# First chunk by channel tile and 128-row filter weights in a hybrid encoder trunk

## The chip, the core and the metric

The kernel runs on one core of one Trainium2 chip. The metric is the device time of one execution in microseconds (us), median of three runs. The engines are TensorE (PE; its weight loads are a row of their own, PEld), VectorE (DVE), ScalarE (ACT), GpSimd (POOL) and SyncE (SP), which here only issues DMAs.

## The reference

Two layers on 256 tokens of 1024 channels, in fp32. Cut to what matters here:

```python
def _rms_norm(x, g):
    return x * lax.rsqrt(jnp.mean(x * x, axis=-1, keepdims=True) + 1e-6) * g

for i in range(2):
    proj = _rms_norm(x, norm_mix_pre[i]) @ w_in[i]
    # three mixers on parts of proj: long convolution by FFT, gated linear attention, pooling
    merged = sum(gate_b * (y_b @ w_br_b[i]) for b in ("hyena", "gla", "pool"))
    x = x + _rms_norm(merged @ w_out[i], norm_mix_post[i])
    # gated MLP with a depthwise convolution of width 3, 1024 -> 2816 -> 1024
    x = x + _rms_norm(mlp(_rms_norm(x, norm_ffn_pre[i])), norm_ffn_post[i])

# the long convolution's filter, positions t, features z (33 wide), hidden width 64:
h = sin(fr2 * (sin(fr1 * (z @ w1 + b1)) @ w2 + b2)) @ w3        # (256, 1024)
h_fwd, h_bwd = h[:, :512] * decay, h[:, 512:] * decay
# y = irfft(rfft(x1 * v) * rfft(filter)); y = x0 * (y + x1 * v * bias)
```

## The kernel before

Products are made of three matmuls in the type float32r: an operand is split into an upper part (a copy in that type, by ACT, helper `act`, L98) and a lower part (the rest, by DVE, helper `tt`, L103), and upper by upper, upper by lower and lower by upper are added in PSUM (helper `mm`, L112). The weights, 162 MB with all else, stream from memory in chunks of 1 MB (128 rows by 2048 numbers, tile `raw`, three buffers), 71 a layer, on SP's queue. Each chunk is split in two halves of 1024 columns (`split_upper`, `split_lower`). A unit of matmuls uses a chunk; between units the kernel lets side chains (generators) step and splits chunks ahead.

A scheduler orders each engine's instructions from dependences and its own idea of durations, except between `open_window` and `close_window`: there PE, DVE and ACT (and POOL in the prologue) run in the order in which the code is written. The prologue is such a window. It reaches into the first units of layer 0.

The prologue works so. SP issues in a row: the first 128 tokens of x as two halves of 512 columns (`load_x(0)`), the norm weights `gcol` as 128 rows of 8 numbers, the first half of chunk 0, the other 128 tokens (`load_x(1)`), the second half of chunk 0, chunk 1 (two halves), chunk 2, and `vec`, the table of per-channel constants. PE runs WARM = 13 matmuls of ones (`rmask`) that nobody reads. For the first tokens ACT squares two halves with row sums (`squares`), DVE makes the mean (`mse`), POOL the root (`rstd`, L369), DVE scales x by it (`normed`, L1212), PE transposes eight tiles of 128 channels (L1215), and `gained` multiplies by the norm weight per channel: ACT writes the upper part, DVE the lower one (`stt`, L106), for four channel tiles at a time. The first chunk's halves are split between these steps. Then the same follows for the other tokens, in the generator `second`, which steps as layer 0 begins. `chunk_x_stationary` is a unit of the first product: x is the stationary operand, and for each of four channel tiles k it issues three matmuls of 128x512: upper by upper (m = 0), upper x by lower weights (m = 1), lower x by upper weights (m = 2). In the very first unit `lows_late` puts the m = 1 ones last in each pair of k, so that they come after the other two.

`filt` makes the long convolution's filter. Its hidden state lies twice in `hs`, the upper part in rows 0 to 63 and the lower part in rows 64 to 127, and the weights `w3` lie twice in 128 rows too. For each of two sets of 128 positions and two directions one matmul takes all 128 rows of `hs` against `w3h`, which is upper and lower state by upper weights, and one takes rows 0 to 63 against `w3l`, the lower weights in 64 rows:

```python
w3h, w3l = big.get([P, DM], F32R), big.get([64, DM], F32R)
tt(w3l[:], kf["w3"][0:64, :], f32(w3h[0:64, :]), ALU.subtract)
mm(ps[:], hs[:, w], w3h[:, c], True, False)
mm(ps[:], hs[0:64, w], w3l[:, c], False, True)
```

Later in a layer the inverse transform of the long convolution takes its matrix in two tiles, loaded by POOL's queue (`in_ih` at L804, `in_il` at L805) when buffers come free. The result of a branch, `y`, is written in upper and lower halves and then multiplied by `w_br`.

Of the kernel before, what the change touches and what calls it, by code (L numbers as in the profile page):

```python
# [18 lines left out]
P = 128  # L19
# [57 lines left out]
def trunk(ctx: ExitStack, tc: tile.TileContext, a: dict, out: bass.AP):  # L77
# [9 lines left out]
    def f32(ap):  # L87
        return ap.bitcast(F32)
# [3 lines left out]
    ahead = {"chunks": 3, "reserve": 0, "at": 0, "quiet": False, "still": False}  # L92
    WARM = 13
    TOKEN = "tables"
# [54 lines left out]
    def load_x(t):  # L149
        for s in HALVES:  # L150
            nc.sync.dma_start(xs[t][:, s], a["x"][t * P:(t + 1) * P, s])  # L151

# [8 lines left out]
    gcol = cpool.tile([P, 8], F32, name="gcol")  # L161
    nc.sync.dma_start(gcol[:], a["gcol"])

# [285 lines left out]
    def filt(i, kf):  # L449
        while len(big.free) < 10:  # L450
            yield
        kf["w3"] = big.get([P, DM])
        w3h, w3l = big.get([P, DM], F32R), big.get([64, DM], F32R)
        kf["dec"] = big.get([P, 2, DH])
# [14 lines left out]
        act(w3h[:], kf["w3"][:])  # L469
        tt(w3l[:], kf["w3"][0:64, :], f32(w3h[0:64, :]), ALU.subtract)  # L470
        sml.put(h2)
# [3 lines left out]
        for t in range(2):  # L475
# [4 lines left out]
            for ps, c in ((pf, slice(0, DH)), (pb, slice(DH, DM))):  # L480
                mm(ps[:], hs[:, w], w3h[:, c], True, False)
                mm(ps[:], hs[0:64, w], w3l[:, c], False, True)
            yield
# [49 lines left out]

    def chunk_x_stationary(n, xt, t, o, half, lows_late=False):

        xth, xtl = xt[0][half], xt[1][half]
        s = slice(t * P, (t + 1) * P)
        todo = [(k, m) for k in range(4) for m in range(3)]
        if lows_late:
            todo.sort(key=lambda km: (km[0] // 2, (0, 2, 1)[km[1]]))  # L540
        for k, m in todo:
            h, l = weights(n, k * 512, 512)
            x = xtl if m == 2 else xth
            mm(o, x[:, k, s], l if m == 1 else h, half == 0 and (k, m) == todo[0], half == 1 and (k, m) == todo[-1])
# [22 lines left out]
    def layer(i, xt, chains):  # L567
# [23 lines left out]
        for at, (n, t) in enumerate(seq):  # L591
# [5 lines left out]
            def fin(t=t, ps=vg_ps[t], dst=(v, sg)[m]):  # L597
# [3 lines left out]
            oldest = min(c for c, _ in seq[at:])  # L601
            unit([nvg[n], nvg[oldest]], lambda: chunk_x_stationary(nvg[n], xt, t, vg_ps[t][:], j, lows_late=i == at == 0),
                 fin if j else None, free=nvg[n] if t else None)
# [600 lines left out]
    def squares(t):  # L1204
        h, ss = big.get([P, DM]), ssq_tile()
        for j, s in enumerate(HALVES):
            act(h[:, s], xs[t][:, s], AF.Square, scale=1.0 / 32.0, accum_out=ss[:, j:j + 1])
        return h, ss

    def normed(t, h, r):  # L1210
        for s in HALVES:
            nc.vector.tensor_scalar_mul(h[:, s], xs[t][:, s], r[:])  # L1212
        ps = [psm.get([P, 2, P]) for _ in range(4)]
        for k in range(8):
            nc.tensor.transpose(ps[k // 2][:, k % 2, :], h[:, k * P:(k + 1) * P], ident[:])  # L1215
        big.put(h)
        return ps

    def gained(t, half, ps):
        s = slice(t * P, (t + 1) * P)  # L1220
        for bank in (0, 1):
            b = ps[half * 2 + bank]
# [6 lines left out]
            psm.put(b)  # L1229

    ps = psm.get([P, P])
    for _ in range(WARM):
# [3 lines left out]
    r0 = rstd_mean(ss0)  # L1236
    split_upper()
    ps0 = normed(0, h0, r0)
    gained(0, 0, ps0)
    split_lower()  # L1240
    h1, ss1 = squares(1)
    r1 = rstd_mean(ss1)
    split_upper()
    load_constants()

    def second():
        ps1 = normed(1, h1, r1)
        yield
        gained(1, 0, ps1)
        gained(0, 1, ps0)  # L1250
        split_half(False)
        split_half(False)
        gained(1, 1, ps1)
        ahead["still"] = False
# [147 lines left out]
```

## Time and profile before

| | before |
|---|---|
| median of three runs | 902.9 us (901.14 to 904.99) |
| the profiled execution | 900.64 us |
| its span, first to last instruction | 898.9 us |
| PE busy | 886.0 us (99%) |
| weight loads busy | 830.5 us (92%) |
| DVE busy | 630.9 us (70%) |
| ACT busy | 505.8 us (56%) |
| POOL busy | 35.0 us (4%) |
| moved by DMA | 164.62 MB, mean 183 GB/s |

The profile is of one execution; 1.7 us of its time lie outside the span. An instruction is named by its line, engine, operation, and the tiles it writes and reads (out<-in, buffer numbers left out); `b`, `s` and `p` are slots of the two pools in SBUF and of the one in PSUM. A timeline row gives the start, the length and the count of instructions that it joins, and in brackets the engine's idle time just before and what ended it.

### The profile page before, as it was taken

The numbers are of one execution on the slowest core, as the hardware profiler recorded it, in microseconds if no ns is written. First come the engines' busy times: TensorE is split into PE (matmuls) and PEld (weight loads), VectorE is DVE, ScalarE is ACT, GpSimd is POOL, SyncE is SP. The second block draws the span as 40 slices with busy tenths as digits, with TensorE's granted clock in tenths as the row PEclk, the third lists the DMA queues.
The fourth block names the chain that finished last, engine by engine and source line by source line (L and its number), as shares of the span: only waits on it lengthen the run. The fifth ranks groups of instructions, "written<-read, shape, count | busy, mean of one in ns | idle before, by whom it ended". The sixth has DMA issues, their size and how long they took to land.

```text
span 898.9 us, 15183 instructions
## 1 busy us (share of the span) xinstructions
PE 886.0 (99%) x6272; PEld 830.5 (92%) x6272; DVE 630.9 (70%) x910; ACT 505.8 (56%) x797; POOL 35.0 (4%) x80
## 2 busy tenths in 40 slices
PE   8999999999999999999999999999999999999997
PEld 6899998999988999998888999999998899999885
DVE  5899979665667698765288888865854967776612
ACT  6778746544355776545167865664542766554511
POOL 3000000100010000000010000000000000000000
PEclk9999999999999999999999999999999999999999
DMA  8853545546537426555439545263743583555601
GB/s 290 343 198 129 187 145 178 197 169 246 196 116 268 156 95 240 182 188 205 170 104 337 181 141 198 96 236 141 245 177 141 189 301 125 183 188 178 221 1 47
DMA packets 26021, 164.62 MB, mean 183 GB/s; under 512 B 3178, under 2 KB 3317, under 8 KB 8032
## 3 DMA queue, kind: packets, MB, share of 16 engines
q1 hardware_dynamic: 22464, 151.70, 47.3%
q0 software_dynamic: 3488, 11.95, 4.1%
q8 instruction: 49, 0.80, 0.4%
q14 instruction: 20, 0.16, 0.1%
HBM read 162.59 MB, written 1.05 MB: 182 GB/s over the span
## 4 chain that ended last, share of the span: by engine, by line
PE 96%; DMA 2%; DVE 2%; issue 0%; ACT 0%; SPq 0%; DVEq 0%; POOLq 0%; ACTq 0%
PE p L112 94%; DMA b<-in_il 1%; DVE b L103 1%; DMA raw<-in_wts 1%; PE p L356 1%; PE p L1132 0%; DVE b L106 0%; PE p L749 0%; PE p L965 0%; ACT b L98 0%; SPq L151 0%; DVE s L923 0%; DVE x L106 0%; DVEq L1398 0%; ACT s L98 0%
## 5 line engine op out<-in xcount | busy, mean ns | idle before, releaser
L112 PE MATMUL p<-b,b 128*128 128x256 f32 (+2 forms) x5958 | 854.2, 304 | 5.3 <-DVE b L103 3.5
L112 PEld LDWEIGHTS p<-b,b 128*128 128x128 f32 x5958 | 794.4, 191 | 55.2 <-DVE b L103 4.8
L103 DVE TENSOR_TENSOR b<-raw,b 128x1024 fp32r<-128x1024 f32 x286 | 342.5, 1216 | 123.6 <-ACT b L98 71.2
L98 ACT ACTIVATE b<-raw 128x1024 fp32r<-128x1024 f32 x288 | 290.9, 1045 | 189.1 <-PE p L112 146.7
L103 DVE TENSOR_TENSOR b<-p,b 128x512 f32<-128x512 f32 (+2 forms) x64 | 40.5, 651 | 63.4 <-ACT s L98 51.6
L98 ACT ACTIVATE s<-p 128x256 f32<-128x256 f32 (+3 forms) x50 | 20.5, 414 | 77.5 <-PE p L112 77.2
L98 ACT ACTIVATE b<-p 128x512 f32<-128x512 f32 (+3 forms) x78 | 43.5, 566 | 30.2 <-PE p L112 20.3
L106 DVE SCALAR_TENSOR_TENSOR s<-p,vec,s 128x255 f32<-128x255 f32 x104 | 49.3, 478 | 6.4 <-ACT s L98 5.5
L98 ACT ACTIVATE s<-p,vec 128x256 f32<-128x256 f32 x52 | 28.8, 557 | 18.7 <-DVE s L106 15.3
L98 ACT ACTIVATE s<-s 128x512 f32<-128x512 f32 (+6 forms) x52 | 27.7, 532 | 13.4 <-DVE s L106 8.2
L103 DVE TENSOR_TENSOR b<-b,b 128x512 f32<-128x512 f32 (+4 forms) x34 | 26.6, 781 | 8.3 <-ACT b L98 7.9
L98 ACT ACTIVATE b<-s 128x512 fp32r<-128x512 f32 x38 | 23.7, 625 | 13.1 <-DVE s L103 13.0
L98 ACT ACTIVATE b<-b 128x512 fp32r<-128x512 f32 (+3 forms) x22 | 16.3, 742 | 24.8 <-DVE b L103 23.6
L103 DVE TENSOR_TENSOR b<-s,b 128x512 fp32r<-128x512 f32 x38 | 25.9, 684 | 5.2 <-ACT b L98 5.2
L103 DVE TENSOR_TENSOR b<-b,p 128x512 f32<-128x512 f32 x24 | 16.3, 684 | 10.1 <-PE p L112 9.9
L98 ACT ACTIVATE b<-b,s 128x128 f32<-128x128 f32 x64 | 20.5, 391 | 1.0 <-DVE s L674 0.9
L106 DVE SCALAR_TENSOR_TENSOR b<-p,vec,b 128x255 f32<-128x255 f32 (+1 forms) x40 | 19.1, 477 | 2.6 <-ACT b L98 2.5
L103 DVE TENSOR_TENSOR s<-s,p 128x512 f32<-128x512 f32 x22 | 15.0, 684 | 8.4 <-ACT s L98 8.0
L109 DVE TENSOR_SCALAR mse<-ssq 128x1 f32<-128x1 f32 (+1 forms) x24 | 4.7, 196 | 18.7 <-ACT s L98 14.9
L103 DVE TENSOR_TENSOR s<-s,s 128x512 f32<-128x512 f32 (+2 forms) x24 | 15.6, 662 | 2.0 <-ACT s L98 2.0
L369 POOL TENSOR_TENSOR rstd<-mse,mhalf 128x1 f32<-128x1 f32 x16 | 8.9, 554 | 209.1 <-DVE mse L109 209.1
L112 PE MATMUL p<-b,s 128*128 128x128 f32 (+1 forms) x80 | 15.7, 315 | 0.0
(95 smaller groups left out, 289.8 us busy)
## 6 DMA issues: line engine op xcount, KB each, us to landing
raw<-in_wts SPq DMA_DIRECT2D x140, 1024.0 KB, 5.0
b<-in_gains POOLq DMA_DIRECT2D x7, 512.0 KB, 6.0
raw<-in_wts SPq DMA_DIRECT2D x4, 512.0 KB, 7.3
b<-in_dft POOLq DMA_DIRECT2D x4, 512.0 KB, 7.0
x<-in_x SPq DMA_DIRECT2D x4, 256.0 KB, 4.4
b<-in_gw POOLq DMA_DIRECT2D x2, 512.0 KB, 5.8
b<-in_fw POOLq DMA_DIRECT2D x2, 512.0 KB, 6.7
b<-in_decay POOLq DMA_DIRECT2D x2, 512.0 KB, 8.0
```

Of the source, the lines that this page charges most:

```text
L98: ins = nc.scalar.activation(o, i, func, **kw)
L103: nc.vector.tensor_tensor(out=o, in0=x, in1=y, op=op)
L106: nc.vector.scalar_tensor_tensor(out=o, in0=x, scalar=s, in1=y, op0=op0, op1=op1)
L109: nc.vector.tensor_scalar(out=o, in0=x, scalar1=s1, scalar2=s2, op0=op0, op1=op1)
L112: ins = nc.tensor.matmul(o, w, x, start=start, stop=stop).ins
L356: nc.tensor.transpose(ps[k // 4][:, k % 4, :], h[:, k * P:(k + 1) * P], ident[:])
L369: nc.gpsimd.tensor_tensor(out=r[:], in0=e[:], in1=mhalf[:, 0:1], op=ALU.pow)
```

## The change

- WARM is 9 instead of 13.
- x is loaded with one DMA for each 128 tokens, whole rows of 4 KB.
- The norm weights are loaded as 8 rows of 128 numbers (`grow`), transposed on PE and copied to `gcol` by DVE.
- Of the squares the first 512 columns are on ACT, the other 512 on DVE.
- The scaling is in three pieces (256, 256, 512 columns) and is separate from the transposes (`scaled`, `turned`).
- Chunk 0 is split in quarters of 512 columns, one per channel tile, each between the norm products of two channel tiles.
- The first unit issues k = 0, 1, 2, then the transposes of the other tokens, then k = 3; within k = 1 to 3 the matmul that needs lower weights comes second to last or last.
- In `second` the upper split of chunk 1's first half comes after `gained(1, 0)`, not before.
- `w3l` has 128 rows, and its matmuls take all 128 rows of `hs`: the product of the two lower parts is added, which the kernel before leaves out.

```diff
--- before.py
+++ after.py
@@ -90,7 +90,7 @@
     LIFT = 1000
     newest = {}
     ahead = {"chunks": 3, "reserve": 0, "at": 0, "quiet": False, "still": False}
-    WARM = 13
+    WARM = 9
     TOKEN = "tables"
     TABLED = (AF.Sin, AF.Exp, AF.Ln, AF.Sigmoid, AF.Gelu)
 
@@ -147,8 +147,7 @@
     HALVES = (slice(0, 512), slice(512, 1024))
 
     def load_x(t):
-        for s in HALVES:
-            nc.sync.dma_start(xs[t][:, s], a["x"][t * P:(t + 1) * P, s])
+        nc.sync.dma_start(xs[t][:], a["x"][t * P:(t + 1) * P, :])
 
     def gain(i, j, eng):
         g = big.get([P, DM])
@@ -159,7 +158,8 @@
     g_cur = {}
     load_x(0)
     gcol = cpool.tile([P, 8], F32, name="gcol")
-    nc.sync.dma_start(gcol[:], a["gcol"])
+    grow = cpool.tile([8, P], F32, name="grow")
+    nc.sync.dma_start(grow[:], a["gains"][0, 0].rearrange("(k c) -> k c", c=P))
 
 
     order = []
@@ -450,7 +450,7 @@
         while len(big.free) < 10:
             yield
         kf["w3"] = big.get([P, DM])
-        w3h, w3l = big.get([P, DM], F32R), big.get([64, DM], F32R)
+        w3h, w3l = big.get([P, DM], F32R), big.get([P, DM], F32R)
         kf["dec"] = big.get([P, 2, DH])
         with tc.issue_after(newest["pool"]):
             nc.gpsimd.dma_start(kf["w3"][:], a["fw3"][i])
@@ -467,7 +467,7 @@
         act(hs[:], h2[:])
         tt(hs[64:P, :], h2[64:P, :], f32(hs[64:P, :]), ALU.subtract)
         act(w3h[:], kf["w3"][:])
-        tt(w3l[:], kf["w3"][0:64, :], f32(w3h[0:64, :]), ALU.subtract)
+        tt(w3l[:], kf["w3"][:], f32(w3h[:]), ALU.subtract)
         sml.put(h2)
         big.put(kf["w3"])
         yield
@@ -479,7 +479,7 @@
             w = slice(t, None, 2)
             for ps, c in ((pf, slice(0, DH)), (pb, slice(DH, DM))):
                 mm(ps[:], hs[:, w], w3h[:, c], True, False)
-                mm(ps[:], hs[0:64, w], w3l[:, c], False, True)
+                mm(ps[:], hs[:, w], w3l[:, c], False, True)
             yield
             hf, hb, u = sml.get([P, DH]), sml.get([P, DH]), sml.get([P, DH])
             tt(hf[:], pf[:], kf["dec"][:, t, :], ALU.mult)
@@ -531,14 +531,17 @@
     def xt_alloc():
         return ([big.get([P, 4, L], F32R) for _ in range(2)], [big.get([P, 4, L], F32R) for _ in range(2)])
 
-    def chunk_x_stationary(n, xt, t, o, half, lows_late=False):
+    def chunk_x_stationary(n, xt, t, o, half, first=None):
+
 
         xth, xtl = xt[0][half], xt[1][half]
         s = slice(t * P, (t + 1) * P)
         todo = [(k, m) for k in range(4) for m in range(3)]
-        if lows_late:
-            todo.sort(key=lambda km: (km[0] // 2, (0, 2, 1)[km[1]]))
+        if first is not None:
+            todo = todo[:3] + [(k, m) for k in range(1, 4) for m in (0, 2, 1)]
         for k, m in todo:
+            if first is not None and (k, m) == (3, 0):
+                first()
             h, l = weights(n, k * 512, 512)
             x = xtl if m == 2 else xth
             mm(o, x[:, k, s], l if m == 1 else h, half == 0 and (k, m) == todo[0], half == 1 and (k, m) == todo[-1])
@@ -599,7 +602,8 @@
                 psm.put(ps)
 
             oldest = min(c for c, _ in seq[at:])
-            unit([nvg[n], nvg[oldest]], lambda: chunk_x_stationary(nvg[n], xt, t, vg_ps[t][:], j, lows_late=i == at == 0),
+            unit([nvg[n], nvg[oldest]], lambda: chunk_x_stationary(nvg[n], xt, t, vg_ps[t][:], j,
+                                                                  chains[1].step if i == at == 0 else None),
                  fin if j else None, free=nvg[n] if t else None)
             if at == (5 if i else 3):
                 close_window()
@@ -1203,22 +1207,27 @@
 
     def squares(t):
         h, ss = big.get([P, DM]), ssq_tile()
-        for j, s in enumerate(HALVES):
-            act(h[:, s], xs[t][:, s], AF.Square, scale=1.0 / 32.0, accum_out=ss[:, j:j + 1])
+        s0, s1 = HALVES
+        act(h[:, s0], xs[t][:, s0], AF.Square, scale=1.0 / 32.0, accum_out=ss[:, 0:1])
+        x = xs[t][:, s1]
+        nc.vector.scalar_tensor_tensor(out=h[:, s1], in0=x, scalar=1.0 / 1024.0, in1=x, op0=ALU.mult, op1=ALU.mult,
+                                       accum_out=ss[:, 1:2])
         return h, ss
 
-    def normed(t, h, r):
-        for s in HALVES:
+    def scaled(t, h, r):
+        for s in (slice(0, 256), slice(256, 512), slice(512, 1024)):
             nc.vector.tensor_scalar_mul(h[:, s], xs[t][:, s], r[:])
+
+    def turned(h):
         ps = [psm.get([P, 2, P]) for _ in range(4)]
         for k in range(8):
             nc.tensor.transpose(ps[k // 2][:, k % 2, :], h[:, k * P:(k + 1) * P], ident[:])
         big.put(h)
         return ps
 
-    def gained(t, half, ps):
+    def gained(t, half, ps, banks=(0, 1)):
         s = slice(t * P, (t + 1) * P)
-        for bank in (0, 1):
+        for bank in banks:
             b = ps[half * 2 + bank]
             of = [(xt[0][half][:, k, s], xt[1][half][:, k, s], b[:, k % 2, :], gcol[:, half * 4 + k:half * 4 + k + 1])
                   for k in (2 * bank, 2 * bank + 1)]
@@ -1228,27 +1237,53 @@
                 stt(xl, src, g, f32(xh), ALU.mult, ALU.subtract)
             psm.put(b)
 
+
+    wh[0], wl[0] = ([big.get([P, 1024], F32R) for _ in range(2)] for _ in range(2))
+
+    def upper(k):
+        act(wh[0][k // 2][:, k % 2 * 512:(k % 2 + 1) * 512], raws[0][:, k * 512:(k + 1) * 512])
+
+    def lower(k):
+        s = slice(k % 2 * 512, (k % 2 + 1) * 512)
+        tt(wl[0][k // 2][:, s], raws[0][:, k * 512:(k + 1) * 512], f32(wh[0][k // 2][:, s]), ALU.subtract)
+
     ps = psm.get([P, P])
     for _ in range(WARM):
         mm(ps[:], rmask[:, 0:P], rmask[:, 0:P], True, True)
     psm.put(ps)
     h0, ss0 = squares(0)
     r0 = rstd_mean(ss0)
-    split_upper()
-    ps0 = normed(0, h0, r0)
-    gained(0, 0, ps0)
-    split_lower()
+    psg = psm.get([P, 8])
+    nc.tensor.transpose(psg[:], grow[:], ident[0:8, 0:8])
+    nc.vector.tensor_copy(gcol[:], psg[:])
+    psm.put(psg)
+    scaled(0, h0, r0)
+    ps0 = turned(h0)
+    upper(0)
+    lower(0)
+    gained(0, 0, ps0, (0,))
+    upper(1)
+    lower(1)
+    gained(0, 0, ps0, (1,))
+    upper(2)
+    lower(2)
     h1, ss1 = squares(1)
     r1 = rstd_mean(ss1)
-    split_upper()
+    upper(3)
+    lower(3)
+    scaled(1, h1, r1)
+    del raws[0]
+    dma_next()
+    state["h"] = state["l"] = 2
     load_constants()
 
     def second():
-        ps1 = normed(1, h1, r1)
+        ps1 = turned(h1)
         yield
         gained(1, 0, ps1)
+        split_upper()
         gained(0, 1, ps0)
-        split_half(False)
+        split_lower()
         split_half(False)
         gained(1, 1, ps1)
         ahead["still"] = False
```

The order that each engine gets changes with it. In the first rows of PE before, `b_5` and `b_8` are the scaled x of the two sets of tokens, `b_6`, `b_9` the upper and `b_7`, `b_10` the lower halves of chunk 0, `b_1`, `b_3` the upper and lower x:

```order
L1215 MATMUL p_5_139<-ident,b_5_123 128x128 x2
L112 MATMUL p_6_180<-b_6_131,b_1_103 128x512 x2
L112 MATMUL p_6_180<-b_6_131,b_3_105 128x512 x2
L112 MATMUL p_6_180<-b_7_132,b_1_103 128x512 x2
L112 MATMUL p_6_180<-b_9_165,b_1_103 128x512 x2
L112 MATMUL p_6_180<-b_9_165,b_3_105 128x512 x2
L112 MATMUL p_6_180<-b_10_166,b_1_103 128x512 x2
L1215 MATMUL p_7_201<-ident,b_8_157 128x128 x2
```

In the kernel after these tiles are `b_9` and `b_10` (scaled x), `b_5`, `b_6` (upper) and `b_7`, `b_8` (lower):

```order
L112 MATMUL p_7_189<-b_7_110,b_1_102 128x512
L112 MATMUL p_7_189<-b_6_109,b_1_102 128x512
L112 MATMUL p_7_189<-b_6_109,b_3_104 128x512
L112 MATMUL p_7_189<-b_8_111,b_1_102 128x512
L1224 MATMUL p_8_199<-ident,b_10_162 128x128 x2
L1224 MATMUL p_9_200<-ident,b_10_162 128x128 x2
L1224 MATMUL p_10_201<-ident,b_10_162 128x128 x2
L1224 MATMUL p_11_202<-ident,b_10_162 128x128 x2
L112 MATMUL p_7_189<-b_6_109,b_1_102 128x512
L112 MATMUL p_7_189<-b_6_109,b_3_104 128x512
```

The eight transposes of the other tokens now stand between the ninth and the tenth matmul of the first unit, and each lower part comes with its own channel tile.

ACT in the prologue before, from its second square on (`raw_80` is chunk 0, `raw_85` chunk 1):

```order
L98 ACTIVATE b_8_157,ssq<-x_68 128x512 x2
L98 ACTIVATE b_9_165<-raw_80 128x1024
L98 ACTIVATE b_14_181<-raw_85 128x1024
L98 ACTIVATE b_1_103<-p_7_201,gcol 128x128 x2
L98 ACTIVATE b_1_103<-p_8_202,gcol 128x128 x2
L98 ACTIVATE b_2_104<-p_4_138,gcol 128x128 x2
L98 ACTIVATE b_2_104<-p_5_139,gcol 128x128 x2
```

And after, where `raw_80` is chunk 0 and `raw_84` chunk 1:

```order
L98 ACTIVATE b_6_109<-raw_80 128x512
L98 ACTIVATE b_10_162,ssq<-x_68 128x512
L98 ACTIVATE b_6_109<-raw_80 128x512
L98 ACTIVATE b_1_102<-p_8_199,gcol 128x128 x2
L98 ACTIVATE b_1_102<-p_9_200,gcol 128x128 x2
L98 ACTIVATE b_14_222<-raw_84 128x1024
L98 ACTIVATE b_2_103<-p_5_138,gcol 128x128 x2
L98 ACTIVATE b_2_103<-p_6_139,gcol 128x128 x2
L98 ACTIVATE b_16_234<-raw_84 128x1024
```

The first split of chunk 1 moved behind the first four norm products of the other tokens, and chunk 0's second half is now two steps with one square between them.

In the middle of layer 0, PE just before the first product of the long convolution's result (`b_121`) with its branch weights, before:

```order
L112 MATMUL p_51_1579<-s_34_1456,s_24_1312 128x256
L112 MATMUL p_52_1652<-b_2_104,b_109_1362 128x256
L112 MATMUL p_55_1754<-b_47_434,b_49_436 128x128 x4
L112 MATMUL p_54_1724<-b_121_1488,b_110_1365 128x256
L112 MATMUL p_57_1772<-b_121_1488,b_110_1365 128x256
L112 MATMUL p_54_1724<-b_122_1489,b_110_1365 128x256
```

And after, where `p_53` is the gate product that was `p_52`, and `p_55` the branch product:

```order
L112 MATMUL p_53_1656<-b_2_103,b_108_1365 128x256
L112 MATMUL p_53_1656<-b_4_105,b_108_1365 128x256
L112 MATMUL p_53_1656<-b_2_103,b_109_1366 128x256
L112 MATMUL p_55_1728<-b_121_1492,b_110_1369 128x256
L112 MATMUL p_56_1758<-b_47_438,b_49_440 128x128 x4
L112 MATMUL p_55_1728<-b_122_1493,b_110_1369 128x256
```

Before, one matmul of the gate's product stands there and the product's 47 others ran earlier; after, it is nineteen in a row, of which the last three are shown.

## Rows read from the trace of the kernel before

**Rows 1.** Page, part 4: shares of the span in the chain that ended last, by engine.
```profile
PE 96%; DMA 2%; DVE 2%; issue 0%; ACT 0%; SPq 0%; DVEq 0%; POOLq 0%; ACTq 0%
```

**Rows 2.** TensorE's waits, whole run: us in total, times, longest us.
```profile
PE p L112 <- DVE b L103: 3.5, 3, 2.2
PE p L112 <- ACT b L98: 1.4, 1, 1.4
...
PE p L112 <- DMA b<-in_il: 0.5, 1, 0.5
```

**Rows 3.** Three stretches: us, each engine's busy us and instructions (x), clock, DMA.
```profile
20.00:60.00 40.00, 40.00 (x258) 35.38 (x256) 34.88 (x53) 29.28 (x39) 1.04 (x2) 1.00 0.82 303
60.00:120.00 60.00, 60.00 (x466) 57.56 (x466) 57.33 (x105) 43.98 (x91) 3.09 (x10) 1.00 0.47 166
146.00:892.00 746.00, 746.00 (x5287) 701.54 (x5286) 505.25 (x689) 403.44 (x612) 22.65 (x44) 1.00 0.51 180
```

**Rows 4.** PE timeline, layer 0's filter: start, length, instruction, count, [idle before].
```profile
58.45 1.70 PE L112 MATMUL p<-b,s 128*128 128x512 f32 x4
...
60.66 1.68 PE L112 MATMUL p<-b,s 128*128 128x512 f32 x4
```

**Rows 5.** The same view, weight loads of the first group.
```profile
58.78 0.19 PEld L112 LDWEIGHTS p<-b,s 64*128 64x128 f32 x1 [0.24 <-issue]
59.22 0.19 PEld L112 LDWEIGHTS p<-b,s 128*128 128x128 f32 x1 [0.25 <-issue]
```

**Rows 6.** Groups by form, whole run: count | busy us, mean ns | idle before, releaser.
```profile
L112 PE MATMUL p<-rmask 128*128 128x128 f32 x26 | 5.9, 425 | 1.2 <-DVE rmask L246 1.2
...
L112 PE MATMUL p<-s 128*128 128x128 f32 x32 | 4.9, 275 | 0.0
...
L103 DVE TENSOR_TENSOR b<-b,b 64x1024 fp32r<-64x1024 f32 x2 | 2.4, 1214 | 1.3 <-ACT b L98 1.3
```

**Rows 7.** Timeline of PE, prologue.
```profile
6.89 1.04 PE L1215 MATMUL p<-ident,b 128*128 128x128 f32 x8
...
18.49 5.78 PE L112 MATMUL p<-b,b 128*128 128x512 f32 x24 [0.16 <-DVE b L103]
```

**Rows 8.** Timeline of ACT and DVE, prologue.
```profile
3.44 0.63 ACT L98 ACTIVATE b<-x 128x512 f32<-128x512 f32 x1 [1.42 <-DMA x<-in_x]
...
7.93 1.06 ACT L98 ACTIVATE b<-raw 128x1024 fp32r<-128x1024 f32 x1 [3.11 <-DMA raw<-in_wts]
...
9.53 1.13 DVE L106 SCALAR_TENSOR_TENSOR b<-p,gcol,b 128x128 fp32r<-128x128 f32 x4 [2.92 <-ACT b L98]
...
13.35 0.88 DVE L1212 TENSOR_SCALAR b<-x,rstd 128x512 f32<-128x512 f32 x2
...
14.48 2.18 ACT L98 ACTIVATE b<-p,gcol 128x128 fp32r<-128x128 f32 x8 [1.35 <-PE p L1215]
...
17.22 1.22 DVE L103 TENSOR_TENSOR b<-raw,b 128x1024 fp32r<-128x1024 f32 x1
```

**Rows 9.** DMA view, windows 2 to 3, 3 to 4 and 4 to 5 us.
```profile
raw<-in_wts SPq DMA_DIRECT2D x1, 512.0 KB, 5.8
...
raw<-in_wts SPq DMA_DIRECT2D x1, 512.0 KB, 6.9
...
q1 hardware_dynamic: 66, 0.25, 97.0%
```

**Rows 10.** Timeline of all engines, end of layer 0's long convolution.
```profile
113.49 0.53 POOL L805 DMA_DIRECT2D b<-in_il  x1 [0.79 <-PE p L112]
...
122.54 14.42 PE L112 MATMUL p<-b,b 128*128 128x256 f32 x118 [0.47 <-DMA b<-in_il]
...
142.74 0.47 DVE L923 TENSOR_SCALAR s<-b,s 128x128 f32<-128x128 f32 x2
...
143.13 0.68 DVE L103 TENSOR_TENSOR b<-b,b 128x512 fp32r<-128x512 f32 x1
...
143.86 2.41 PE L112 MATMUL p<-b,b 128*128 128x256 f32 x18 [2.16 <-DVE b L103]
```

## Prediction

> **What bounds the kernel now.** I read the chain of waits first: 96% of it is TensorE (PE) [rows 1]. The view of what PE waits for comes next; the reader is to see how little is left: 3.5 us behind lower halves written by VectorE (DVE), 1.4 behind ScalarE (ACT), 0.5 behind one DMA [rows 2], and 1.2 before its first instruction [rows 6]. From 146 to 892 it is busy throughout [rows 3]: all these waits lie before. So an edit can bring three things only: less time of PE's own instructions, a smaller wait among those few, or (as a loss) a new wait. DVE is the engine that could make one: it is busy 34.88 us of the 40 from 20 to 60, and 57.33 of the 60 from 60 to 120 [rows 3]. The profiled execution took 900.64 us, the median of the runs is 902.9; I sum against the first and scale the result by 902.9/900.64.
>
> **The filter on 128 rows.** Each layer has two groups of four 128x512 matmuls, alternately with 128 rows and with 64. The first group begins at 58.45, and the second, with four 256-wide matmuls between, at 60.66: 2.21 us [rows 4]. Ordinary 128x512 matmuls follow each other by 0.234: 24 of them last 5.78, and (5.78-0.39)/23 leaves out the last one's length [rows 7]; 256-wide ones step by 14.42/118 = 0.122 [rows 10]. So the stretch should take 4x0.234 + 4x0.122 = 1.42, and 0.79 is lost. The loads show where: ahead of the second one, of 64 rows, and of the third, of 128, stands 0.24 and 0.25 of idle with no releaser but issue, and the loads of the other groups read alike [rows 5]. Four groups at 0.8 make 3.2 us, with bounds of 2.4 (two and a half such gaps a group, 0.6) and 3.8 (0.24 at each of sixteen loads). On DVE the lower half of these weights was 64x1024 and took 1.21 us a piece; a 128x1024 one takes 1.22 [rows 6, 8], so the added rows cost nothing there. PE is continuous at this place, so the saving reaches the end unless DVE falls behind (a rival).
>
> The row is the evidence: the idle comes and goes with the number of rows. [...]
>
> **The prologue.** Its end is the point from which PE is continuous: 18.49, when DVE's lower part of chunk 1's first half (17.22, 1.22 long) is done [rows 7, 8]. Back from there stand eight DVE products, ACT's eight from 14.48, eight transposes, the scaling at 13.35 and the squares. All that PE does before 18.49 fits in gaps, so an earlier first matmul is worth nothing by itself. Step by step, for the kernel after:
> - x by whole rows. The first square starts at 3.44 on half the row now; with one transfer I put it at 4.0 (the second half's place). ACT's takes 0.63 and needs its sum read, and DVE's, beside it, I take at 0.68, like its 128x512 step [rows 10]: both end at 4.87, and before two squares in a row from 3.44 ended hardly sooner. Nothing. The bounds of DVE's square are 0.44 (half of the pair of scalings, 0.88) and 0.88 [rows 8].
> - Norm weights by a transpose: one PE transpose, one DVE copy, in the time in which DVE waits for POOL's root. Nothing; under 0.44, one scaling, if that cover were gone [rows 8]. What goes is one DMA on SP's queue ahead of the weights.
> - First weights. Their first half lands 5.8 us after its issue, just ahead of ACT's step at 7.93, the second 6.9 us after its own (at 10.43) [rows 8, 9]. From 4 to 5 us the engines were 97% busy with 66 packets and only 0.25 MB, so it is not small packets that filled them [rows 9]. I take 7.7 and 10.26, 0.2 for the issue that is gone; the early bound is a rival.
> - ACT: a quarter of the upper part 0.56 (half of 1.06, with overhead), two norm products 0.56 (2.18 for eight) [rows 8]. From 7.72: quarter, products, quarter, products to 9.96; third quarter from 10.28 to 10.84; square (0.6) to 11.45; fourth to 12.0.
> - DVE: a quarter 0.64 (half of 1.22, with overhead), two products 0.57 (1.13 for four) [rows 8]. They follow ACT: 8.34 to 10.74; third quarter 10.9 to 11.54; square to 12.22. Root and hand-overs 0.85: scaling at 13.1, against 13.35. It comes in pieces, so the transposes start at 13.45, and ACT's products at 14.05, against 14.48.
> - Then the order gives the lead back: ACT does four products (to 15.15), a half chunk that before was split ahead of them (to 16.15), four products (to 17.2). DVE's eighth product ends at 17.5 and the lower part at 18.7. PE is continuous from 18.8: 0.3 later than 18.49.
>
> So the prologue costs 0.3. Bounds: a loss of 1.5 (transfers 1.0 later, as the two halves differ in their time to landing, and DVE's square at 0.88), a gain of 1.8 (weights that land early). Code that only waits behind other things: `ngb` is put ahead of four products on DVE and waits for `vec`; that DMA no longer stands behind as much, and DVE has waits there; nothing.
>
> **The order in the middle.** The scheduler's order changes as well. Eight matmuls of 0.122 (14.42/118) that stood ahead of the inverse transform now stand behind it. Its second matrix is sent for at 113.49, when PE frees a buffer at the same place in both kernels, so PE reaches it 0.97 earlier and the wait of 0.47 at 122.54 becomes 1.44. In return 0.98 more work stands before the wait of 2.16 at 143.86, for the DVE step at 143.13; and a DVE pair of 0.47 that ran just ahead of that step now runs behind it [rows 10]. That leaves 0.71; one more DVE step, of 0.68, goes ahead of a split there, and I take 0.4. Net 2.16-0.4-0.97 = 0.8 saved; bounds 1.0 lost (nothing gained at the second place) and 2.2 saved. Further on both orders agree up to the end but for the widths in layer 1's filter.
>
> **Sum.** 3.2 + 0.8 - 0.3 = 3.7 saved: 900.64-3.7 = 896.94, scaled 899.2.
>
> **Rivals.**
> [...]
> B, the first weights land early: the small transfer and three issues gone, the stream moves faster than 0.25 MB a microsecond [rows 9], the first half is there before ACT needs it, and by the same steps the second scaling comes at 11.35 rather than 13.1. The prologue gains 1.5 instead of losing 0.3: 5.5 saved, 897.4. Against it: the slow stretch before 8 us does not look like a matter of packet size.
> C, the other side, DVE becomes the bound. It gets about 1.7 us more in the prologue (two squares 1.36, four quarters for two halves 0.28, a copy) and from 20 to 60 it has 40-34.88 = 5.1 idle to take it up. If order and waits eat that, layer 0's filter gains nothing (PE then waits for lower halves), 1.74 appears as waits before 120, and the middle gives only its loss of 1.0: 1.6-1.74-0.3-1.0 = 1.4 lost, 904.4. It decides once DVE runs over 5.1 late at 60.
> D, the width does nothing: the idle at each load belongs to the change of what is read, not of the rows. 3.2 less: 0.5 saved, 902.4. The alternation of rows with an idle at each step [rows 5] speaks against it.
>
> **How the numbers follow.** Chances: forecast 0.42, A 0.20, B 0.20, C 0.08, D 0.05, rest 0.05. A measurement tells about 0.5%, 4.5 us, from no change: below 898.4 is faster, above 907.4 slower. The forecast's own bounds reach below 898.4 in a third of its cases (0.14), B in most (0.16), the others 0.04: faster 0.34; slower 0.04 from the worst of C and the rest; the same 0.62. The range, 895.4 to 902.9, takes in B with the middle's bound of 2.2 (897.4-1.4 = 896.0) and a little of the filter's, and on the other side A and D; it leaves out C and the rest.
>
> **What would show it.** Filter groups: eight rows of 128x512 with steps near 0.23 and no idle at loads; if 0.43 stays, D. [...] A wait near 1.4 for the second inverse matrix and a wait under 0.8 after 135. Any new wait for a lower half between 19 and 120 is C. The prediction is wrong if PE waits after 146, or if instructions that the edit does not touch change in length.

## The result and the profile after

| | before | after |
|---|---|---|
| median, six runs each | 902.76 us | 895.89 us (894.96 to 896.90) |
| ratio to before, 95% interval | | 0.9922 (0.9907 to 0.9938) |
| the profiled execution | 900.64 us | 895.14 us |
| its span | 898.9 us | 893.4 us |
| PE busy | 886.0 us | 882.0 us |

The forecast was 3.7 us less and 899.2; it became 6.9 less by the medians and 5.5 by the two profiled executions. The sign was right, the size not.

What PE waits for in the kernel after, us in total, times, longest (before: [rows 2]):

```profile
PE p L1224 <- DVE b L1219: 2.9, 2, 1.8
PE p L112 <- DVE rmask L246: 1.2, 1, 1.2
PE p L112 <- DVE b L103: 0.5, 1, 0.5
PE p L112 <- ACT b L98: 0.3, 1, 0.3
```

The first row is the prologue, where PE waits for scaled x. The wait for the second inverse matrix is gone, and so is the one of 2.2 for a lower half; one of 0.3 is new, at 78 us.

PE's timeline of the filter after (start, length, instruction, count):

```profile
59.06 1.55 PE L112 MATMUL p<-b,s 128*128 128x512 f32 x6
60.44 2.67 PE L112 MATMUL p<-b,b 128*128 128x256 f32 x21
...
65.22 0.62 PE L112 MATMUL p<-b,s 128*128 128x512 f32 x2
```

The same view, weight loads of the first six:

```profile
58.94 1.24 PEld L112 LDWEIGHTS p<-b,s 128*128 128x128 f32 x6
```

Against [rows 4, 5]: six matmuls take 1.38 up to the next start, 0.23 each, and the loads run without the idle of 0.24. The scheduler split one group, so two stand by themselves.

PE's timeline of the prologue after, against [rows 7]:

```profile
6.70 1.94 PE L1224 MATMUL p<-ident,b 128*128 128x128 f32 x8 [1.10 <-DVE b L1219]
8.29 3.14 PE L112 MATMUL p<-b,b 128*128 128x512 f32 x9
13.24 1.23 PE L1224 MATMUL p<-ident,b 128*128 128x128 f32 x8 [1.80 <-DVE b L1219]
14.22 3.92 PE L112 MATMUL p<-b,b 128*128 128x512 f32 x16
18.65 5.74 PE L112 MATMUL p<-b,b 128*128 128x512 f32 x24 [0.51 <-DVE b L103]
```

Five rows of ACT and DVE from the same stretch, against [rows 8]:

```profile
6.41 0.63 ACT L98 ACTIVATE b<-raw 128x512 fp32r<-128x512 f32 x1 [1.20 <-DMA raw<-in_wts]
...
9.40 0.63 ACT L98 ACTIVATE b<-raw 128x512 fp32r<-128x512 f32 x1 [0.35 <-DMA raw<-in_wts]
...
12.74 1.01 DVE L1219 TENSOR_SCALAR b<-x,rstd 128x256 f32<-128x256 f32 x3 [0.45 <-POOL rstd L369]
...
13.69 1.15 ACT L98 ACTIVATE b<-p,gcol 128x128 fp32r<-128x128 f32 x4 [2.51 <-PE p L1224]
...
17.38 2.35 DVE L103 TENSOR_TENSOR b<-raw,b 128x1024 fp32r<-128x1024 f32 x2
```

Both halves of chunk 0 arrive earlier (6.41 and 9.40 instead of 7.9 and 10.4), the second scaling comes 0.6 earlier, and yet the lower part that ends the prologue starts at 17.38, where before it was 17.22: between lie the half chunk and the eight products in their new order on ACT. Both profiles have 49 of these 128x512 matmuls up to the end of their last row (4+8+13+24 and 9+16+24), at 18.49+5.78 = 24.27 and 18.65+5.74 = 24.39: a loss of 0.12.

At the end of layer 0's long convolution, against [rows 10], PE (two rows) and the DVE step for which it waited 2.16 before:

```profile
138.66 3.53 PE L112 MATMUL p<-b,b 128*128 128x256 f32 x28
...
138.91 0.68 DVE L103 TENSOR_TENSOR b<-b,b 128x512 fp32r<-128x512 f32 x1
```

PE has work throughout; there is no idle. So the profiled executions differ by 3.2 (filter) + 2.16 + 0.47 (two waits) - 0.12 (prologue) - 0.28 (new wait) = 5.4 of the 5.5. The other 1.4 of the medians is not in these two profiles; the experiments point to where it lies.

### The profile page after: what moved, and what is told of

The parts are those of the page before. It is cut to its first block, busy times and chain, and to the rows that moved or that the text cites. A ratio compares the mean times of both kernels' runs of the same rounds, so it can differ in the third digit from the quotient of the medians.

```text
span 893.4 us, 15182 instructions
## 1 busy us (share of the span) xinstructions
PE 882.0 (99%) x6265; PEld 830.3 (93%) x6265; DVE 632.4 (71%) x919; ACT 505.0 (57%) x795; POOL 35.4 (4%) x80
## 3 DMA queue, kind: packets, MB, share of 16 engines
HBM read 162.59 MB, written 1.05 MB: 183 GB/s over the span
## 4 chain that ended last, share of the span: by engine, by line
PE 96%; ACT 1%; DMA 1%; DVE 1%; SPq 0%; issue 0%; POOL 0%; DVEq 0%; POOLq 0%; ACTq 0%
PE p L112 95%; ACT b L98 1%; DMA raw<-in_wts 1%; PE p L356 1%; PE p L1136 0%; ACT s L98 0%; DVE b L103 0%; PE p L969 0%; PE p L753 0%; POOL rstd L369 0%; DVE b L106 0%; SPq L150 0%; DVE x L106 0%; DVEq L1433 0%; DVE b L1213 0%
## 5 line engine op out<-in xcount | busy, mean ns | idle before, releaser
L103 DVE TENSOR_TENSOR b<-raw,b 128x1024 fp32r<-128x1024 f32 (+2 forms) x288 | 342.6, 1209 | 123.4 <-ACT b L98 69.1
L98 ACT ACTIVATE b<-raw 128x1024 fp32r<-128x1024 f32 (+2 forms) x290 | 291.3, 1041 | 179.8 <-PE p L112 143.6
L155 POOL DMA_DIRECT2D b<-in_gains x7 | 3.8, 550 | 269.3 <-PE p L112 157.6
```

What stands on the lines that cost most here:

```text
L98: ins = nc.scalar.activation(o, i, func, **kw)
L103: nc.vector.tensor_tensor(out=o, in0=x, in1=y, op=op)
L155: eng.dma_start(g[:], bass.AP(src.tensor, src.offset + (i * 4 + j) * DM, [[0, P], [1, DM]]))
```

## Experiments

Times are medians beside the kernel before on the same chip, whose median went from 900.9 to 902.6 with the chip, so ratios are compared. The ratios are those on record; the quotient of the two medians differs from them by up to 0.0015.

**The filter alone.** In the kernel before:

```diff
-        w3h, w3l = big.get([P, DM], F32R), big.get([64, DM], F32R)
+        w3h, w3l = big.get([P, DM], F32R), big.get([P, DM], F32R)
...
-                mm(ps[:], hs[0:64, w], w3l[:, c], False, True)
+                mm(ps[:], hs[:, w], w3l[:, c], False, True)
```

> The kernel before with the filter's lower weights on 128 rows and nothing else; every engine's order is that of before. My theory (the switch between 64 and 128 rows costs about 0.2 us a matmul): steps of 0.23 in the four groups, 3.2 us less, 899.6 by the median of before of 902.8; the waits at the second inverse matrix (0.5) and after 141 us (2.2) stay. [...] Rival (DVE takes it back): steps of 0.23, but a new wait for a lower half before 120 us.

Measured: 898.13 against 901.87, ratio 0.9946 (0.9932 to 0.9960). PE's timeline of the two groups:

```profile
57.82 1.09 PE L112 MATMUL p<-b,s 128*128 128x512 f32 x4
58.74 0.64 PE L112 MATMUL p<-b,b 128*128 128x256 f32 x4
59.22 1.09 PE L112 MATMUL p<-b,s 128*128 128x512 f32 x4
```

From group to group 1.40, before 2.21: 0.81 saved, four times 3.2. Nothing was taken back; the waits in the middle (2.2 and 0.4) are as before. The whole time fell by more than 3.2 (3.7 by the medians, 3.6 to 6.1 by the ratio's interval). In this profile the prologue, too, ends 0.6 earlier (17.89 against 18.49), as the first weights came at 7.34 instead of 7.93; so the starts of the groups measure the filter, and the whole time does not.

**The price of the switch.** The kernel before, the same four matmuls in another order:

```diff
                 mm(ps[:], hs[:, w], w3h[:, c], True, False)
+            for ps, c in ((pf, slice(0, DH)), (pb, slice(DH, DM))):
                 mm(ps[:], hs[0:64, w], w3l[:, c], False, True)
```

> The kernel before with the four matmuls of each filter group in another order: two of 128 rows, then two of 64, instead of alternating. If the price is one of a change in the number of rows, two changes a group instead of four: half of the 3.2 us goes, 1.6 less, and the idle of 0.24 ahead of loads stands at two loads of a group. If a 64-row matmul is slow by itself, the idle stays at four loads or sits at the same two matmuls and nothing is saved. The scheduler's order differs a little elsewhere, so the loads are the measure, not the whole time.

Measured: 899.99, ratio 0.9986 (0.9972 to 0.9999). Weight loads:

```profile
58.71 0.31 PEld L112 LDWEIGHTS p<-b,s 64*128 64x128 f32 x2 [0.35 <-issue]
59.37 0.53 PEld L112 LDWEIGHTS p<-b,b 128*128 128x128 f32 x4 [0.35 <-issue]
60.51 0.31 PEld L112 LDWEIGHTS p<-b,s 64*128 64x128 f32 x2 [0.36 <-issue]
61.18 1.97 PEld L112 LDWEIGHTS p<-b,b 128*128 128x128 f32 x16 [0.36 <-issue]
```

Two matmuls of 64 rows in a row, and idle only where the number of rows changes: twice a group instead of four times, 0.35 each. The groups begin at 58.15 and 59.95, 1.80 apart, 0.41 less than 2.21. The price is one of the change, not of a 64-row matmul.

**All but the filter.** The changed kernel with `w3l` on 64 rows:

> The changed kernel with the filter's lower weights on 64 rows again; every engine's order is that of the changed kernel. Theory: the steps of 0.43 are back and 3.2 us with them, 895.9 + 3.2 = 899.1; the waits in the middle of layer 0 stay away. So the rest of the change is worth 902.8 - 899.1 = 3.7, nearly all from the two waits of 0.5 and 2.2. Rival: the filter alone explains the whole gain and the rest is nothing, about 902.8.

Measured: 898.73, ratio 0.9958 (0.9944 to 0.9972). By the medians filter and rest add up: 3.74 and 3.14 are 6.9, the whole. By the ratios they are 4.9 and 3.8 against 7.0, each with an interval of about 1.3 either way, which allows the sum but does not confirm it. The profile shows neither of the two waits in the middle, but something new, in the view by stretches (us, busy time and count of PE, PEld, DVE, ACT, POOL, granted clock, DMA share, GB/s):

```profile
14.00:17.50 3.50, 3.50 (x12) 2.93 (x12) 2.34 (x10) 3.50 (x10) 3.34 (x7) 0.51 0.97 311
```

The granted clock is 0.51 there (in stretches of half a microsecond 0.50 from 14.5 to 17, and 1.00 from 4 to 14 and from 17.5 to 21). PE had been idle for 1.74 up to 13.37, waiting for the second scaling. The first filter group begins at 59.95 instead of 59.06 in the same order of work: 0.9 lost in this execution, of which 0.13 stood already ahead of the second transposes (13.37 against 13.24).

**Thirteen warm-ups** in the changed kernel (WARM = 13):

> The changed kernel with 13 warm-up matmuls again. [...]

Measured: 895.42, ratio 0.9919 (0.9905 to 0.9934): no difference. With the four matmuls the first eight transposes take 1.23 instead of 1.94, at a granted clock of 1.00 in both profiles, and that brings nothing that these runs show. But here, too, the granted clock fell, in the second pause (0.66 from 13 to 13.5, 0.50 from 13.5 to 16.5, 1.00 ahead of it):

```profile
13.00:17.00 4.00, 3.53 (x13) 3.18 (x14) 2.38 (x9) 2.83 (x9) 4.00 (x8) 0.57 0.88 321
```

The filter begins at 59.80, 0.7 later than in the changed kernel's profile; 0.23 of that stood ahead of the second transposes (13.47 against 13.24).

**The pause filled**, in the changed kernel:

```diff
     def second():
+        ps = psm.get([P, P])
+        for _ in range(7):
+            mm(ps[:], ident[:], ident[:], True, True)
+        psm.put(ps)
         ps1 = turned(h1)
```

> The changed kernel with seven more matmuls that nobody reads (128x128 of the identity, about 1.5 us) between the ninth matmul of the first unit and the transposes of the other tokens, where PE pauses from 11.4 to 13.2. Theory: in some executions this pause drops the clock to the lower level from 13 to 17.5 (two of three profiles of this order showed it, with the end of the prologue 0.7 to 0.9 later); with the pause filled the granted clock stays at 1.00 from 10 us on in the profile, the median falls by 0.3 to 0.6 to about 895.4. Rival: the prologue's end hangs on DVE and the lower clock costs nothing on the whole: the same median, 895.9. The other way: the extra matmuls hold the transposes up, 0.2 later.

Measured: 898.91, ratio 0.9967 (0.9955 to 0.9979), slower than the changed kernel by 3 us (medians, on two chips) or 4 (ratios). The prologue did as expected: the granted clock is 1.00 from 4 to 21 us, and the lower part's wait ends at 18.25. But the scheduler answered the added matmuls with another order in the middle: one gate matmul ahead of the first branch matmul, as in the kernel before, and the wait is back:

```profile
141.26 4.94 PE L112 MATMUL p<-b,b 128*128 128x256 f32 x39 [2.16 <-DVE b L103]
```

That was not intended and told the most. Over all fourteen profiles of this document, the seven with nineteen gate matmuls in a row there have no such wait, and the seven with a single one have it.

**Two that differ by one dummy.** The filter-alone kernel with four, and with five, matmuls that nobody reads ahead of the other tokens' transposes; with five the scheduler chooses the nineteen:

```diff
-        for _ in range(4):
+        for _ in range(5):
             mm(warm[:], ident[:], ident[:], True, True)
         ps1 = normed(1, h1, r1)
```

> The kernel before with the 128-row filter and four matmuls that nobody reads (0.22 us each) ahead of the other tokens' transposes. The scheduler's order in the middle of layer 0 is as before: one gate matmul ahead of the first branch matmul. Theory (the order in the middle is worth 2 to 2.6 us by itself): the waits of 2.2 after 141 us and of about 0.4 for the second inverse matrix are there; 898.1 of the kernel with the filter alone plus up to 0.9 for the four: 898.1 to 899.0.

> The same with five such matmuls. On the chip that is 0.22 us more, but the scheduler now puts nineteen gate matmuls in a row ahead of the first branch matmul, as in the changed kernel, though nothing else of its prologue is there. Theory: the wait of 2.2 after 141 us is gone and the one for the second inverse matrix too; 2 to 2.6 us faster than the one with four, about 896.3. Rival (the gain of the middle comes from the new prologue, not from the order): 0.2 slower than the one with four.

Measured: 900.69, ratio 0.9978 (0.9968 to 0.9989), with four; 896.16, ratio 0.9934 (0.9922 to 0.9947), with five. PE's waits for others between 24 and 150 us, with four:

```profile
122.52 14.42 PE L112 MATMUL p<-b,b 128*128 128x256 f32 x118 [0.20 <-DMA b<-in_il]
143.85 6.41 PE L112 MATMUL p<-b,b 128*128 128x256 f32 x39 [2.17 <-DVE b L103]
```

and with five:

```profile
79.25 10.14 PE L112 MATMUL p<-b,b 128*128 128x256 f32 x78 [0.26 <-ACT b L98]
```

So the middle's gain comes with the order and needs nothing of the new prologue. But the step is 4.5 (4.0 by the ratios), not 2 to 2.6. Much of the rest is in the same profile of the one with four: after its wait the granted clock falls (1.00 up to 144.5, 0.50 from 145 to 148, 1.00 from 148.5).

```profile
143.85:147.85 4.00, 4.00 (x21) 4.00 (x22) 3.51 (x9) 2.66 (x3) 0.00 (x0) 0.60 0.52 141
```

21 matmuls in four microseconds at a mean clock of 0.60; the kernel before has 33 in the four after its wait, at 1.00, so twelve of 0.122 are missing, 1.5 us. The granted clock also fell in the prologue (0.51 from 11.5 to 15), and the prologue ends 0.5 later than with five dummies (20.37 against 19.86); that part is not the middle's. Together 0.20 + 2.17 + 1.5 + 0.5 - 0.26 = 4.1 of the 4.45 by which these two profiled executions differ; the other 0.3 is not accounted for.

**The kernel before, twice more.**

> The kernel before once more, for a second profile: its executions spread over 4 us (899.6 to 903.9), and the first profile was of one near the lower end. If it is the prologue that spreads, the point from which PE is continuous (18.49 in the first profile) moves by a microsecond or more, with the landing of the first weights or with the clock; otherwise the waits of the middle (0.5 and 2.2) are what moves.

Measured: 901.94. The prologue is much as in the first profile, as are the waits in the middle, and one more stands in layer 1:

```profile
599.14 0.94 PE L112 MATMUL p<-b,s 128*128 128x128 f32 x6 [1.19 <-ACT s L98]
```

ACT was late there behind a weight chunk (it waited 2.22 for it at 596.33, and in the first profile did not wait for it). Why the chunk was late I have not found.

> The kernel before a third time, for one more profile. The profile of the kernel with four extra matmuls shows the clock at the lower level for 3.8 us right after the wait of 2.2 at 143.85. Theory: this happens to the kernel before too, in some of its executions. If this execution takes over 902, its profile shows a granted clock below 1.00 between 143 and 149 or between 7 and 18, or a wait like the 1.2 at 599; if it takes 900 to 901, none of them. Rival: an execution over 902 shows none of these, and the spread has another cause.

Measured: 903.45, and the profile shows the drop in both places, the prologue (0.50 from 12 to 15) and behind the wait in the middle (0.50 from 145.5 to 148). By half-microsecond stretches each lasts 3.4 us, and so does the one with four dummies, not 3.8. Stretches of 10 us of this execution:

```profile
10.00:20.00 10.00, 8.72 (x33) 6.15 (x32) 7.60 (x20) 7.45 (x22) 5.70 (x11) 0.83 0.98 318
140.00:150.00 10.00, 7.83 (x55) 7.63 (x54) 10.00 (x21) 7.63 (x16) 0.00 (x0) 0.83 0.40 126
```

of the first profile of the same kernel:

```profile
10.00:20.00 10.00, 8.69 (x39) 6.11 (x38) 8.80 (x21) 8.65 (x22) 5.69 (x11) 1.00 0.96 315
140.00:150.00 10.00, 7.84 (x67) 7.64 (x66) 10.00 (x19) 6.78 (x12) 0.00 (x0) 1.00 0.58 186
```

and of the kernel after:

```profile
10.00:20.00 10.00, 7.68 (x36) 5.67 (x36) 8.09 (x21) 7.49 (x20) 5.61 (x11) 1.00 0.94 319
140.00:150.00 10.00, 10.00 (x87) 10.00 (x85) 10.00 (x17) 6.98 (x10) 0.00 (x0) 1.00 0.73 255
```

With the drop PE does 55 matmuls instead of 67 in the same ten microseconds around the wait: 12 x 0.122 = 1.5 us on top of the wait's 2.16. In the kernel after there is no idle there, and the granted clock is 1.00. PE in the prologue of this execution (in the first profile the four start at 9.29 after 1.36 of idle, and the eight take 2.38):

```profile
9.62 1.41 PE L112 MATMUL p<-b,b 128*128 128x512 f32 x4 [2.32 <-ACT b L98]
12.17 3.58 PE L112 MATMUL p<-b,b 128*128 128x512 f32 x8 [1.15 <-DVE b L103]
```

The filter begins 1.49 later than in the first profile (59.94 against 58.45); 0.33 of that stood ahead of the first row (9.62 against 9.29), so up to 1.2 is left for the drop.

**Parts of the prologue.** The changed kernel with the norm weights by 128 short rows, without transpose and copy:

> The changed kernel with the norm weights loaded as 128 rows of 32 bytes again, at the same place of SP's queue, without transpose and copy. Theory (the small rows hold the first weights up): ACT starts on the first weights at 7.2 or later instead of 6.4, as in the kernel before (7.3 to 7.9). Rival (whole rows of x and the earlier issue did it): it stays at 6.4 to 6.6. In either case the time moves little, up to 0.5 us, since the second token half's way through DVE ends the prologue.

Measured: 896.42, ratio 0.9935 (0.9912 to 0.9957). ACT starts on the first weights earlier still:

```profile
5.65 0.63 ACT L98 ACTIVATE b<-raw 128x512 fp32r<-128x512 f32 x1 [0.62 <-DMA raw<-in_wts]
```

My theory fell: the short rows don't hold the weights up. The lower part's wait ends at 18.22 in this profile, 0.43 earlier than in the changed kernel's, so the transpose is no gain that these runs show.

The changed kernel with x in halves:

> The changed kernel with x loaded in halves of 512 columns again. Theory: the first half lands about 1 us earlier (3.4 instead of 4.4) but the pair of squares waits for the second, so nothing before 4.3 changes; the first weights start 0.4 to 0.8 us later than 6.4, as two more issues of 0.43 stand ahead. Rival: the 2-KB packets are slow themselves and the first weights come past 7.2. Time within 0.5 us of the changed kernel's.

Measured: 896.51, ratio 0.9943 (0.9921 to 0.9965). The first weights come at 7.52 instead of 6.41, and the wait ends 1.05 later:

```profile
19.70 4.60 PE L112 MATMUL p<-b,b 128*128 128x512 f32 x19 [0.51 <-DVE b L103]
```

Of the 1.1, 0.47 is the issue: with one DMA more ahead, the first weights are sent for at 2.07 instead of 1.60. Over the fourteen profiles ACT starts on them at 5.65 to 6.73 in the six with whole rows and at 7.34 to 8.25 in the eight with halves, so loading x whole brings them early; how much of it is the longer rows and how much the issue was not tried apart. By the whole time neither can be told from the changed kernel.

**A kernel that may beat both.** The changed kernel with 11 warm-ups and the pause filled in a form that keeps the nineteen:

```diff
-    WARM = 9
+    WARM = 11
...
+        for _ in range(fill):
+            mm(ps[0][:, 0, :], ident[:], ident[:], True, True)
...
-        ps1 = turned(h1)
+        ps1 = turned(h1, 7)
```

> The changed kernel with 11 warm-up matmuls and seven matmuls that nobody reads in the pause before the other tokens' transposes, in a form for which the scheduler keeps the nineteen gate matmuls in a row. Theory: no drop of the clock between 13 and 17.5, no wait of 2.2 after 141; 0.3 to 0.8 faster than the changed kernel's 895.9 (by ratio to before 0.9915). Rival: the drop costs nothing on the whole, ratio 0.992 as for the changed kernel.

Measured: 895.12 (894.70 to 895.27), ratio 0.9920 (0.9906 to 0.9933). The granted clock is 1.00 from 4 to 880 us and there is no wait in the middle, and its four runs lie closer together than others, but the ratio is that of the changed kernel: not shown to be faster.

## Why the prediction was right or wrong

**The filter: right.** 0.8 a group and 3.2 in all was the forecast, 0.81 a group the measurement. Rival D falls. The loads last 0.19 at 64 and at 128 rows [rows 5], so the loss is not in the loads' own time. It is in the idle where the number of rows changes: 0.24 and 0.25 in the kernel before [rows 5], 0.35 in the grouped order, where two alike follow each other without it. What in TensorE takes that time no run here shows.

**The prologue: right in sum, by steps that were off.** A loss of 0.3 was forecast, 0.12 came in the profile. I had the first half of chunk 0 at 7.7 and it came at 6.41; the second at 10.26, and it came at 9.40. Rival B had the first half there before ACT needs it. That was met in part (ACT still waited 1.20 for it), and the gain of 1.5 did not come: the second half and the square behind it still set the second scaling, and what was gained there (12.74, forecast 13.1) was lost in ACT's new order, as the forecast's last step said. The total came close to B's 897.4, but for another reason.

**The clock: a loss without a term in the sum.** Rival A, which has 0.20 of the chances and with D the upper side of the range, has PE slow through the prologue after nine warm-ups. Its price was my estimate, and no run shows it: in the kernel after the first eight transposes are slower (1.94, 1.04 before), but sixteen 128x512 matmuls from 14.22 take 3.92, 0.24 each as before, the granted clock is 1.00 from 4 to 21, and thirteen warm-ups bring no time back. What the runs show in its place is a granted clock of 0.50 for 3.4 us around the pause ahead of the second transposes: two of the five profiles of kernels with this pause have it (with the filter undone, with thirteen warm-ups), with the filter 0.7 to 0.9 later. It isn't a loss of the change alone: the kernel before has pauses there too and showed the drop in one of three profiles.

**The middle: the step that failed.** The forecast was 0.8 saved; the first two profiles show 2.63 from the two waits, less the new wait near 80 us (0.28; 0.26 to 0.28 in all seven profiles with the nineteen). The comparison of four and five dummies shows more with what the clock adds. Three terms were off.
- The wait for the second inverse matrix was to grow to 1.44, with the transfer held at 9.0 us to landing. It took 6.4. In the DMA view of the microsecond in which it is issued, before:

```profile
raw<-in_wts SPq DMA_DIRECT2D x1, 1024.0 KB, 9.0
b<-in_il POOLq DMA_DIRECT2D x1, 512.0 KB, 9.0
```

and after:

```profile
raw<-in_wts SPq DMA_DIRECT2D x1, 1024.0 KB, 6.1
b<-in_il POOLq DMA_DIRECT2D x1, 512.0 KB, 6.4
```

  A weight chunk moves beside it in both, and both transfers are shorter after. Kernels with one gate matmul show 7.6 to 9.1 for it, those with nineteen 6.0 to 7.1. I carried the time to landing over as if it were the transfer's own, and in these rows it goes with the order. The weight chunk beside it is sent for 0.22 ahead of it before (113.27 and 113.49) and 0.58 ahead after (111.98 and 112.56). That this makes the difference is argued from these rows, not tried.
- The wait of 2.16 was to keep 0.4, and kept nothing. The forecast counted eight matmuls, 0.98 us, as new work ahead of it; it was eighteen. PE from the six `s,s` matmuls on that stand there in both kernels, before:

```profile
136.80 0.88 PE L112 MATMUL p<-s,s 128*128 128x256 f32 x6
137.52 2.61 PE L112 MATMUL p<-b,b 128*128 128x256 f32 x21
```

  and after:

```profile
132.97 0.88 PE L112 MATMUL p<-s,s 128*128 128x256 f32 x6
133.69 4.77 PE L112 MATMUL p<-b,b 128*128 128x256 f32 x39
```

  The DVE step for which PE waits starts 6.33 behind the first of the six before (143.13) and 5.94 after (138.91). So the eighteen, 2.2 us, stand in PE's way and not in DVE's. If eight of them came from ahead of the second matrix, as the forecast has it, the other ten stood between that and the six, and the forecast left them out.
- A wait was priced at its length. In two of the seven profiles with this wait the granted clock falls behind it (0.59 and 0.60 over four microseconds), and 1.5 more is lost. That is most likely the part of the medians' 6.9 that the first two profiles lack: both are of executions without a drop. Each execution has its mean granted clock on record. Of the 49 of the kernel before that were timed beside the experiments, fourteen have 0.999 and took 899.6 to 901.1 us; the other 35 have 0.993 to 0.997 and took 901.3 to 905.3. Of the six of the kernel after, two have 0.999 (895.0 and 895.1), four 0.995 or 0.996 (895.7 to 896.9). At 0.999 the medians lie 5.3 apart (900.4 and 895.1), close to the 5.5 of the two profiles. So most executions of before had a drop, and it cost more there than after. In which stretch it fell, a mean does not tell; one further execution of before (901.94 at 0.998) was late by the wait at 599 instead.

**DVE as the bound** did not come: between 60 and 120 it is busy 59.10 of 60, and PE's only wait there is 0.28.

So the measured time lies at the low end of the range because the middle was worth about three times what I gave it, and because of the granted clock, for which no term of the sum stood. That the range held is in part luck: its low end was worked out from B's gain, which did not come, and from the middle's bound of 2.2, which was passed. By the forecast's own mark (below 898.4 is faster, chance 0.34) the less likely outcome came. The rule behind it: I treated a reordering by the scheduler as a side effect with bounds of 1.0 lost and 2.2 saved and took a value in between, where the rows of the order (nineteen matmuls of 0.122 against one, 2.2 us of cover) spoke for the upper end.

## What to carry to other kernels

A wait of the matmul engine can cost more than its length, and in only some executions: here, in two of seven profiles, 1.5 us on top of 2.2, with a granted clock of 0.59 and 0.60 over the four microseconds behind it. So look at several profiles, and at the granted clock of each execution, before a median is explained from one. Where a scheduler simulates the program to set its order, an edit in the prologue can decide an order 120 us later; compare the orders at the places of known waits, and price a change of order there by all the work that it puts between the start of the chain that ends the wait and the wait itself. Keep the row count of neighbouring matmuls alike: here each change between 64 and 128 rows cost about 0.2 us of TensorE (0.81 a group with four changes, 0.41 of it with two fewer), and the wider operand 0.01 of VectorE (1.21 at 64 rows, 1.22 at 128).

## What the hardware showed that was not expected

- The granted clock fell from 1.00 to 0.50 around pauses of 1.1 to 2.3 us (idle of 2.32 ahead of 9.62, 1.15 ahead of 12.17 and 2.17 ahead of 145.21 in the third profile of before; 1.74 ahead of 13.37 with the filter undone), and stayed at 1.00 in others with pauses as long (2.16 ahead of 143.86 in the first profile of before, 1.80 ahead of 13.24 in the kernel after).
- With x in whole rows of 4 KB instead of halves, ACT could start on the first weights, the transfer behind it in the same queue, 1.1 us earlier (6.41 against 7.52), though as many bytes stood ahead of it; 0.47 of that is its earlier issue. 128 rows of 32 bytes ahead of it made it no later (5.65).
